# Nine first-layer projections in plain fp32, scan angles in turns, and a new issue order of both mixers

## The chip, the core and the metric

The kernel runs on one core of a Trainium2 chip. The core has five engines that work side by side: TensorE (PE, the matrix engine; its weight loads are shown as PEld), VectorE (DVE), ScalarE (ACT), GpSimd (POOL), and SyncE (SP), which here only issues DMAs. Each engine takes its own instructions strictly in the order in which they stand in its queue, and waits on semaphores where an operand comes from another engine or from a DMA. The metric is the device time of one execution in microseconds (us), as the median of several runs.

## The reference

A two-layer decoder trunk on a sequence of 512 tokens of width 1024, batch 1. Each layer normalises `x`, multiplies it by one wide input projection, feeds slices of the result to three mixers (a sparse attention called NSA, a low-rank attention called MLA, and a diagonal state-space scan called S5), joins them by an output projection, and then runs a gated feed-forward network with a short convolution. Cut to what matters here:

```
cos, sin = rope_angles(positions)
for l in range(DEPTH):                                   # DEPTH = 2
    h = rms_norm(x, attn_norm[l])
    (q_a, k_c, v_c, k_s, v_s, k_w, v_w, gate_a,
     c_q, c_kv, k_r, u) = split(h @ w_in[l])             # 16 column tiles of 128
    o_a = nsa_attention(q_a, k_c, v_c, k_s, v_s, k_w, v_w, gate_a, ...)
    o_b = mla_attention(c_q, c_kv, k_r, cos, sin, ...)
    o_c = s5_ssm(u, ...)
    x = x + concat[rms_norm(o_a), rms_norm(o_b), rms_norm(o_c)] @ w_out[l]
    x = x + conv_ffn(rms_norm(x), ...)
out = rms_norm(x)

# in s5_ssm: the scan's decay is a complex number per group and state
dt = exp(log_dt);  a_bar = exp((a_re + 1j * a_im) * dt)   # angle a_im * dt, up to many turns
```

All data is float32. `rope_angles` needs the sine and cosine of position times frequency; the scan needs the sine and cosine of multiples of `a_im * dt`.

## The kernel before

**Layout.** Activations are kept transposed, features on the 128 partitions and the 512 tokens along the free dimension, so `x` is eight tiles of 128x512. The input projection is 16 tiles of 128 output features, named `u0 u1 ckv krg cq0 cq1 cq2 kc vc ks kw vs vw q0 q1 q2`; each takes eight 128x128 weight blocks, loaded as two halves of 128x512 (256 KB).

**Precision by splitting.** Nearly every large matmul is done in a reduced float format (`fp32r`) on split operands: `split` (lines 224 to 231) writes a rounded `hi` and the rest `lo`; ACT makes `hi` (line 226, or line 229 with a scale), DVE or POOL makes `lo` (line 227, or line 230 with a scale). `mm3` (lines 239 to 242) then adds three products: hi by hi, hi by lo, lo by hi. A weight half is loaded by `wload` into one of three `raw` tiles and split into one of four `wt` tiles; for the input projections POOL makes the weights' `lo` (`win="G"`). A few matmuls are plain float32 on unsplit operands: the sums of squares (line 253), the broadcast of `rstd` (line 271), the transposes, the compression (line 816), and one 128x512 product in `k_rope` (line 764).

**The start.** Eight chunks of `x` are loaded; each is scaled and split at once by `prep_x` (lines 313 to 318), while the halves of the first two projections (`vc`, `kc`) arrive between them. The squares of `x` are added up on POOL (line 294), PE sums them over partitions (line 253), DVE runs the short chain of `rstd_` (lines 256 to 268), PE broadcasts its result (line 271), and ACT copies it to SBUF (line 275). Each finished projection is multiplied by that `rstd` as DVE takes it out of PSUM (lines 687 and 689), so projections may run before `rstd` is known, in a ring of four PSUM banks, but cannot leave PSUM before.

**The tables.** `trig` (lines 300 to 312) brings an angle into -pi to pi: DVE multiplies by 1/(2 pi) and rounds by a magic number (lines 301, 302), subtracts three parts of 2 pi (line 304), clips (line 305); ACT takes the sine of the angle and of half of it (lines 308, 309), and DVE makes the cosine as 1 - 2 sin^2 (lines 310, 311). It is used once for the rotary tables (`rope`, 128x512) and, in `ssm_tables` of each layer, for a 128x16, a 128x256 and two 128x512 tiles. The first layer's tables run at the start of its mixer (task `tab`); the second layer's run inside the first layer's feed-forward network.

**The mixers.** A layer's mixer is a list of tasks. `PLAN0` and `PLAN1` order them: a task with step -1 is issued before the first head; the others are issued at a step of the head pipeline, and some are tied behind a given PE instruction of a head. A head unit (18 in all: 12 NSA units, two per head, then 6 MLA units) goes through `prep`, `scores` (PE, line 519; taken out of PSUM by DVE with a row minimum, line 520; exponentials on ACT, line 523), `scale` (POOL, line 532) and `pv` (transposes on PE, line 544; splits by ACT and DVE, lines 226 and 227; products on PE, line 548). The tasks named here: `cmp0` and `cmp1` compress keys and values, `ca` scores them, `pa0` to `pa3` and `sp0` to `sp3` prepare and spill the scan's matrices by quarters (lines 410 to 427 and 440 to 453, first layer only), `s0` to `s3` run the scan, `w0` to `w7` are the first parts of the output projection. The tile framework's scheduler merges these lists into one queue for each engine, so the final order of an engine is read from the built program, not from the table; `high_priority(offset=cfg["hp"])` moves `rstd_` forward in it.

Of the kernel before, what the change touches and what calls it, by code (L numbers as in the profile page):

```python
# [13 lines left out]
AF = mybir.ActivationFunctionType  # L14
OP = mybir.AluOpType
# [10 lines left out]
PI = float(np.nextafter(np.float32(math.pi), np.float32(0)))  # L26
MAGIC = 1.5 * 2.0 ** 23
# [103 lines left out]
def _pre(names):  # L131
# [3 lines left out]
# The order in which each layer's mixer is issued. An entry is (task, step of the head pipeline, instruction of the  # L135
# tensor engine that it stays behind as (stage, unit) or None); step -1 comes before the first head.
PLAN0 = _pre('vc kc q2 cmp0 q0 tab krg q1 rope cmp1 ks kw pa0 vs sp0 gates pa1 ca sp1 pa2 sp2 pa3 sp3 ') + (
# [3 lines left out]
    ("mlav", 8, None), ("so1", 9, None), ("glu", 11, None), ("mixc", 11, None), ("mixe", 15, None),  # L141
    ("w0", 16, (0, 13)), ("w1", 17, (1, 14)), ("w2", 17, (3, 13)), ("w3", 17, (0, 14)), ("w4", 19, (1, 16)),
    ("w5", 20, (3, 15)))
PLAN1 = _pre('krg q1 kc q0 vc gates q2 cmp0 ks ca u0 kw cp ') + (
# [3 lines left out]
    ("mlav", 8, None), ("glu", 11, None), ("krope", 11, None), ("mixc", 16, None), ("mixe", 16, None),  # L148
    ("w0", 17, (3, 13)), ("w1", 18, (0, 15)), ("w2", 19, (1, 16)), ("w3", 19, (3, 15)), ("w4", 20, (3, 16)))
# [6 lines left out]
def tile_trunk(ctx, tc, xT_in, pos, cst_in, small_in, win, wuq, wuk, wuv, wglu, wout, wup, wdn,  # L156
# [450 lines left out]
    for c in range(8):  # L607
# [4 lines left out]
        for i, at in enumerate(cfg["lead"]):  # L612
            if at == c:
                first[heads2[i % 2]].append(wproj(0, heads2[i % 2], i // 2))
# [708 lines left out]
```

## Time and profile before

| | us |
|---|---|
| median of 3 runs | 1373.47 |
| lowest and highest run | 1370.69, 1375.71 |
| profiled execution: span from first to last instruction | 1372.3 |
| PE busy in it | 1302.4 (95%) |
| DVE, ACT, POOL busy | 856.5 (62%), 638.8 (47%), 724.4 (53%) |
| first rows: first head's scores on PE, and taken out by DVE | 105.5, 112.0 |
| first layer's feed-forward network, roughly | 340 to 725 |
| second layer's mixer, roughly | 725 to 1008 |

The profile is of one execution. Busy time of an engine counts its instructions from start to end; matmuls are pipelined, so one that takes 0.39 us from start to end may be followed 0.23 us later by the next. `PEclk` is the clock that TensorE was granted, as a share of 2.4 GHz; there are two levels, 2.4 and 1.2 GHz, so a mean of 0.75 in a stretch means half of it at each. The idle time shown beside an instruction is that of its engine just before it, with the instruction or DMA that ended it.

### The profile page before, as it was taken

What the parts mean: (1) busy time and instruction counts of PE and PEld (TensorE: products, weight loads), DVE (VectorE), ACT (ScalarE), POOL (GpSimd) and SP (SyncE); (2) the same over time, 40 slices, a digit from 0 to 9 for tenths busy, and PEclk for the clock granted to TensorE, in tenths of its full rate; (3) what the DMA queues carried; (4) which work ended last, traced back from release to release, by engine and by line L of the source; (5) the groups of instructions that cost most, each with busy time, mean ns of one, the idle gap of its engine ahead of it and who ended that gap; (6) DMA issues with size and microseconds to landing.
All of it is one profiled execution on the core that took longest, in us unless ns stands there. A gap on an engine that the chain in (4) does not pass through costs nothing.

```text
span 1372.3 us, 19205 instructions
## 1 busy us (share of the span) xinstructions
PE 1302.4 (95%) x6414; PEld 1079.2 (79%) x6414; DVE 856.5 (62%) x1733; ACT 638.8 (47%) x1322; POOL 724.4 (53%) x722
## 2 busy tenths in 40 slices
PE   7888989998998999999999999999999999999997
PEld 5676777786876888888888887877878888888886
DVE  6988889858695334643466488986764433442455
ACT  4334667754443233423443356886453323332344
POOL 7485546654759155545437665556376315612532
PEclk9989999999999999999999999999999999999998
DMA  6243622212333333443353433121223333333332
GB/s 224 83 131 99 182 85 66 68 62 64 98 99 113 111 95 100 117 124 95 112 173 112 149 124 106 59 60 43 83 85 106 95 100 99 94 92 106 95 94 83
DMA packets 91556, 140.14 MB, mean 102 GB/s; under 512 B 15553, under 2 KB 36545, under 8 KB 91457
## 3 DMA queue, kind: packets, MB, share of 16 engines
q1 hardware_dynamic: 90176, 134.72, 32.2%
q0 software_dynamic: 1280, 4.20, 1.0%
q8 instruction: 50, 0.82, 0.3%
q14 instruction: 50, 0.40, 0.1%
HBM read 125.01 MB, written 15.96 MB: 103 GB/s over the span
## 4 chain that ended last, share of the span: by engine, by line
PE 72%; DVE 19%; issue 3%; POOL 2%; ACT 2%; DMA 2%; SPq 0%; DVEq 0%; POOLq 0%; ACTq 0%
PE bank L240 21%; PE bank L241 20%; PE bank L242 20%; DVE r L227 3%; PE bank L519 2%; PE bank L548 2%; DVE f L520 2%; PE bank L544 2%; DVE r L230 1%; DVE f L304 1%; DVE f L1157 1%; PE bank L271 1%; PE bank L816 1%; PE bank L253 1%; POOL wt L227 1%
## 5 line engine op out<-in xcount | busy, mean ns | idle before, releaser
L240 PE MATMUL bank<-r,wt 128*128 128x512 f32 x1466 | 580.9, 397 | 15.2 <-ACT wt L226 7.3
L241 PE MATMUL bank<-r,wt 128*128 128x512 f32 x1466 | 577.0, 394 | 4.4 <-DVE r L230 3.6
L242 PE MATMUL bank<-r,wt 128*128 128x512 f32 x1466 | 573.4, 394 | 5.1 <-POOL wt L227 5.1
L227 POOL TENSOR_TENSOR wt<-raw,wt 128x512 fp32r<-128x512 f32 (+2 forms) x272 | 355.0, 1309 | 300.1 <-ACT wt L226 291.0
L226 ACT CAST wt<-raw 128x512 fp32r<-128x512 f32 (+2 forms) x398 | 231.0, 584 | 332.5 <-PE bank L241 189.6
L240 PEld LDWEIGHTS bank<-r,wt 128*128 128x128 f32 x1466 | 278.2, 190 | 77.2 <-ACT wt L226 8.9
L242 PEld LDWEIGHTS bank<-r,wt 128*128 128x128 f32 x1466 | 278.0, 190 | 66.1 <-POOL wt L227 8.5
L241 PEld LDWEIGHTS bank<-r,wt 128*128 128x128 f32 x1466 | 278.4, 190 | 62.8 <-DVE r L230 6.5
L227 DVE TENSOR_TENSOR wt<-raw,wt 128x512 fp32r<-128x512 f32 (+3 forms) x126 | 88.9, 709 | 51.7 <-ACT wt L226 51.3
L294 POOL TENSOR_TENSOR f<-f,f 128x512 f32<-128x512 f32 (+1 forms) x53 | 68.0, 1284 | 99.9 <-ACT f L286 98.4
L532 POOL TENSOR_SCALAR f<-f,sml 128x128 f32<-128x128 f32 (+3 forms) x144 | 79.3, 569 | 52.2 <-DVE sml L530 18.0
L227 DVE TENSOR_TENSOR r<-bank,r 128x256 fp32r<-128x256 f32 (+4 forms) x196 | 90.2, 476 | 24.2 <-ACT r L226 23.0
L1182 DVE TENSOR_TENSOR f<-bank,f 128x512 f32<-128x512 f32 x44 | 30.3, 690 | 112.6 <-PE bank L242 103.1
L1188 POOL TENSOR_TENSOR f<-f,f 128x512 f32<-128x512 f32 x44 | 58.0, 1320 | 74.6 <-ACT f L1187 74.6
L523 ACT ACTIVATE f<-f,sml 128x384 f32<-128x384 f32 (+3 forms) x144 | 80.6, 560 | 32.5 <-DVE sml L520 31.6
L226 ACT CAST r<-bank 128x256 fp32r<-128x256 f32 (+4 forms) x196 | 79.0, 417 | 31.8 <-PE bank L544 15.7
L548 PE MATMUL bank<-r,r 128*128 128x512 f32 (+3 forms) x288 | 82.1, 353 | 10.4 <-DVE r L227 7.5
L519 PE MATMUL bank<-r,r 128*128 128x128 f32 (+3 forms) x336 | 79.3, 339 | 9.8 <-DVE sml L520 9.5
L226 ACT CAST r<-f 128x512 fp32r<-128x512 f32 (+1 forms) x76 | 46.9, 620 | 80.5 <-DVE f L1189 65.7
L520 DVE CUSTOM_DVE_ANT_0 f<-bank,cst 128x384 f32<-128x384 f32 (+3 forms) x144 | 67.8, 481 | 12.7 <-PE bank L519 11.6
L1189 DVE TENSOR_TENSOR f<-bank,f 128x512 f32<-128x512 f32 x44 | 30.4, 690 | 72.7 <-POOL f L1188 68.9
L1217 DVE TENSOR_TENSOR f<-bank,f 128x512 f32<-128x512 f32 x48 | 32.7, 688 | 65.6 <-PE bank L242 65.5
(225 smaller groups left out, 1549.9 us busy)
## 6 DMA issues: line engine op xcount, KB each, us to landing
raw<-in_wup_dram SPq DMA_DIRECT2D x176, 256.0 KB
raw<-in_wdn_dram SPq DMA_DIRECT2D x72, 256.0 KB
raw<-in_win_dram SPq DMA_DIRECT2D x64, 256.0 KB
f<-pd SPq DMA_DIRECT2D x32, 256.0 KB
raw<-in_wout_dram SPq DMA_DIRECT2D x32, 192.0 KB
f<-in_xT_dram SPq DMA_DIRECT2D x16, 256.0 KB
f<-in_w_dram SPq DMA_DIRECT2D x16, 256.0 KB
pd<-f SPq DMA_DIRECT2D x16, 256.0 KB
```

Of the source, the lines that this page charges most:

```text
L226: A.copy(hi, src)
L227: (E or V).tensor_tensor(lo, src, f32(hi), op=OP.subtract)
L240: PE.matmul(p, lhsT=w[:, 0, o:o + n], rhs=x[:, 0], start=start, stop=False)
L241: PE.matmul(p, lhsT=w[:, 0, o:o + n], rhs=x[:, 1], start=False, stop=False)
L242: PE.matmul(p, lhsT=w[:, 1, o:o + n], rhs=x[:, 0], start=False, stop=stop)
L294: G.tensor_tensor(a, a, q, op=OP.add)
L519: PE.matmul(p[:, :w], lhsT=q[:, i * 128:w], rhs=k[:, :w], start=n == 0, stop=n == len(passes) - 1)
L520: V.tensor_tensor_reduce(out=sm[i], in0=p[:, :w], in1=C("mask")[:, 512 - w:], op0=OP.add, op1=OP.min, scale=1.0, scalar=3.0e38, accum_out= ...
L523: A.activation(sm[i], sm[i], AF.Exp, bias=mx[:, i:i + 1], scale=-1.0, accum_out=su[:, i:i + 1])
L532: G.tensor_scalar(sm[i], sm[i], rs[:, i:i + 1], 1.0, op0=OP.mult, op1=OP.mult)
L548: PE.matmul(o[:, j * 128:], lhsT=v[j], rhs=pr[:, x, :w], start=first and j == 0 and x == 0, stop=last and j == 3 and x == 1)
L1188: G.tensor_tensor(t, t, r_f, op=OP.mult)
```

## The change

Four things change.

1. **Plain fp32 projections.** Nine projections of the first layer (`vc kc q2 q0 krg q1 ks kw vs`, the list `plain`) are computed as one plain float32 matmul for each weight block, on the weight as loaded (`wplain`, straight into a free `f` tile) and on the scaled `x` (`xg`, made by ACT). The other seven, and the second layer, keep `mm3`. The split `hi`, `lo` of `x`, which these need, is now made by `split_x` from `xg`, in program order after `q2`.
2. **Angles in turns.** `turn_trig` takes the scan's angle as a fraction of a circle: DVE rounds by the magic number and subtracts (two instructions), and ACT takes the sine, the absolute value, and the sine of a quarter turn less that value. `trig`, now used for the rotary tables alone, keeps its reduction but takes the cosine in the same way.
3. **Issue order.** `PLAN0` and `PLAN1` are new, `hp` is 0 instead of 50, and the places behind which two late output tiles of the first layer stand differ.
4. **One engine.** The `lo` part of the MLA queries (made by `split` in `proj_q` after line 940; `q="V"`) moves from POOL to DVE, six 128x512 instructions in each layer.

```diff
+TURN = 2 * PI
-PLAN0 = _pre('vc kc q2 cmp0 q0 tab krg q1 rope cmp1 ks kw pa0 vs sp0 gates pa1 ca sp1 pa2 sp2 pa3 sp3 ') + (
+PLAN0 = _pre('vc kc cmp0 tab q0 rope q2 krg cmp1 ks pa0 kw q1 sp0 pa2 gates pa1 vs sp1 ca sp2 pa3 sp3 ') + (
...
-PLAN1 = _pre('krg q1 kc q0 vc gates q2 cmp0 ks ca u0 kw cp ') + (
+PLAN1 = _pre('krg q0 vc gates q2 ks kc cmp0 q1 ca u0 kw ') + (
...
-CFG = dict(plan=(PLAN0, PLAN1), F=dict(main=15, aux=10, side=12), R=dict(main=16, side=3, q=3, pr=2), nraw=3, nw=4, hp=50,
+CFG = dict(plan=(PLAN0, PLAN1), F=dict(main=15, aux=10, side=12), R=dict(main=16, side=3, q=3, pr=2), nraw=3, nw=4, hp=0,
...
+           ... plain=("vc", "kc", "q2", "q0", "krg", "q1", "ks", "kw", "vs"), splitat="q2", ...
-           eng=dict(..., q="G", xadd="V"))
+           eng=dict(..., q="V", xadd="V"))
...
         A.activation(s, ang, AF.Sin)
-        A.activation(k, ang, AF.Sin, scale=0.5)
-        V.tensor_tensor(k, k, k, op=OP.mult)
-        V.tensor_scalar(k, k, -2.0, 1.0, op0=OP.mult, op1=OP.add)
+        A.activation(k, ang, AF.Abs)
+        A.activation(k, k, AF.Sin, bias=quarter, scale=-1.0)
+
+    def turn_trig(u, k, s):
+        V.tensor_scalar(k, u, MAGIC, None, op0=OP.add)
+        V.scalar_tensor_tensor(u, k, MAGIC, u, op0=OP.subtract, op1=OP.subtract)
+        if s is None:
+            return
+        A.activation(s, u, AF.Sin, scale=-TURN)
+        A.activation(k, u, AF.Abs)
+        A.activation(k, k, AF.Sin, bias=quarter, scale=-TURN)
...
-        V.tensor_tensor(th, aim, dt, op=OP.mult)
-        trig(th, kk, None)
+        V.scalar_tensor_tensor(th, aim, 1.0 / (2 * math.pi), dt, op0=OP.mult, op1=OP.mult)
+        turn_trig(th, kk, None)
...
+    def wplain(name, kh):
+        raw = F.get()
+        SY.dma_start(raw, win[0, TILES.index(name), :, kh * 512:(kh + 1) * 512])
+        return raw
+
+    def split_x():
+        for c in range(8):
+            pr = R.get("main")
+            split(xg[c], pr[:, 0], pr[:, 1])
+            hx.append(pr)
+
     for c in range(8):
         xt = F.get()
         SY.dma_start(xt, xT_in[c])
-        prep_x(xt, c, hx, None, 0, "attn")
+        g = F.get()
+        A.activation(g, xt, AF.Identity, scale=S(0, "attn", c))
+        xg.append(g)
...
+            for kh in range(2 if plain else 0):
+                w = first[name].pop(0) if first.get(name) else wplain(name, kh)
+                for k in range(4):
+                    PE.matmul(p, lhsT=w[:, k * 128:(k + 1) * 128], rhs=xg[kh * 4 + k], start=kh + k == 0, stop=kh == 1 and k == 3)
+                F.free(w)
```

How the engines' queues change is read from the built programs. The first place is PE at the end of the first two projections (`vc` in `bank_151`, `kc` in `bank_152`; `ones` is the sum of squares, `bank_153` the third projection; `r` and `wt` are split tiles, `f` plain ones). Before:

```order
L241 MATMUL bank_152<-r_106,wt_130 128x512
L242 MATMUL bank_152<-r_106,wt_130 128x512
L240 MATMUL bank_152<-r_107,wt_130 128x512
L241 MATMUL bank_152<-r_107,wt_130 128x512
L242 MATMUL bank_152<-r_107,wt_130 128x512
L253 MATMUL bank_155<-ones,f_71 128x1 x4
L253 MATMUL bank_155<-ones,f_72 128x1 x4
L242 MATMUL bank_153<-r_100,wt_127 128x512
L240 MATMUL bank_153<-r_101,wt_127 128x512
```

And the same place of the changed program:

```order
L703 MATMUL bank_152<-f_78,f_76 128x512
L703 MATMUL bank_151<-f_80,f_73 128x512
L703 MATMUL bank_152<-f_80,f_76 128x512
L703 MATMUL bank_151<-f_82,f_73 128x512
L703 MATMUL bank_152<-f_82,f_76 128x512
L257 MATMUL bank_155<-ones,f_83 128x1 x4
L257 MATMUL bank_155<-ones,f_84 128x1 x4
L703 MATMUL bank_153<-f_64,f_63 128x512
L703 MATMUL bank_153<-f_68,f_63 128x512
```

The sum of squares stands behind 50 split matmuls before (48 of the two projections and two of the third) and behind 16 plain ones now. The second place is POOL at the start (line 227, now 231: a weight's `lo`; line 294, now 298: the sum of squares). Before:

```order
L227 TENSOR_TENSOR wt_128<-raw_125,wt_128 128x512
L294 TENSOR_TENSOR f_71<-f_71,f_73 128x512
L294 TENSOR_TENSOR f_72<-f_72,f_74 128x512
L227 TENSOR_TENSOR wt_129<-raw_126,wt_129 128x512
L992 MEMSET f_66 128x64 x2
L294 TENSOR_TENSOR f_71<-f_71,f_75 128x512
L294 TENSOR_TENSOR f_72<-f_72,f_76 128x512
L992 MEMSET f_67 128x64 x2
L623 TENSOR_SCALAR smt<-smt 128x2 x2
L227 TENSOR_TENSOR wt_130<-raw_124,wt_130 128x512
```

Changed:

```order
L298 TENSOR_TENSOR f_83<-f_83,f_85 128x512
L298 TENSOR_TENSOR f_84<-f_84,f_86 128x512
L298 TENSOR_TENSOR f_83<-f_83,f_87 128x512
L298 TENSOR_TENSOR f_84<-f_84,f_85 128x512
L650 TENSOR_SCALAR smt<-smt 128x2 x2
L298 TENSOR_TENSOR f_84<-f_84,f_87 128x512
L298 TENSOR_TENSOR f_83<-f_83,f_86 128x512
L231 TENSOR_TENSOR wt_127<-raw_124,wt_127 128x512
L231 TENSOR_TENSOR wt_128<-raw_125,wt_128 128x512
```

No weight split stands among the sums of squares any more. The third place is DVE while it makes the scan's tables and takes projections out of PSUM (`f_98`, `f_92` are the two 128x512 angle tiles, `f_93`, `f_99` their scratch; line 416, now 429, is the scan's first small operand). Before:

```order
L301 TENSOR_SCALAR f_93<-f_92 128x512
L302 TENSOR_SCALAR f_99<-f_99 128x512
L416 TENSOR_SCALAR f_95<-f_95,cst 128x64
L417 TENSOR_SCALAR f_95<-f_95 128x64
L364 TENSOR_TENSOR ar<-f_97,f_96 128x256
L302 TENSOR_SCALAR f_93<-f_93 128x512
L304 SCALAR_TENSOR_TENSOR f_98<-f_99,f_98 128x512
L369 TENSOR_SCALAR sml_139<-ar 128x16
L823 TENSOR_SCALAR f_88<-f_88 128x62
L304 SCALAR_TENSOR_TENSOR f_92<-f_93,f_92 128x512
L687 SCALAR_TENSOR_TENSOR f_85<-bank_152,f_79 128x512
L304 SCALAR_TENSOR_TENSOR f_98<-f_99,f_98 128x512
```

Changed, at about the same place (the second angle tile is made and reduced, lines 399, 317 and 318):

```order
L728 TENSOR_TENSOR f_87<-bank_151,f_85 128x512
L439 TENSOR_TENSOR f_96<-f_95,ais 128x512
L399 SCALAR_TENSOR_TENSOR f_92<-f_95,cst 128x512
L440 TENSOR_TENSOR f_97<-f_97,f_96 128x512
L317 TENSOR_SCALAR f_93<-f_92 128x512
L860 TENSOR_SCALAR f_88<-bank_158,smt 128x62
L318 SCALAR_TENSOR_TENSOR f_92<-f_93,f_92 128x512
L841 TENSOR_TENSOR f_90<-f_86,f_89 64x256 x2
L430 TENSOR_SCALAR f_95<-f_95 128x64
L439 TENSOR_TENSOR f_96<-f_95,ai 128x512
```

Each angle tile now takes two DVE instructions after it is made, where it took six before the sine and two after it; the scan's quarter products (lines 439 and 440) follow sooner. Up to the first head's scores both programs issue the same 11 projections.

## Rows read from the trace of the kernel before

**Rows 1.** The page: the chain that ended last, by engine.

```profile
PE 72%; DVE 19%; issue 3%; POOL 2%; ACT 2%; DMA 2%; SPq 0%; DVEq 0%; POOLq 0%; ACTq 0%
```

**Rows 2.** Busy time by stretch; the first row names the columns.

```profile
core 0: us, PE busy (x) PEld busy (x) DVE busy (x) ACT busy (x) POOL busy (x), PEclk, DMA share, GB/s
...
27.70:112.00 84.30, 73.14 (x363) 60.87 (x363) 77.17 (x157) 29.86 (x51) 55.59 (x63) 0.94 0.37 114
112.00:320.00 208.00, 190.54 (x1071) 158.22 (x1072) 165.65 (x470) 133.84 (x348) 113.60 (x148) 0.96 0.30 90
...
725.00:1008.00 283.00, 270.75 (x1493) 228.38 (x1493) 216.42 (x544) 168.79 (x408) 169.29 (x192) 1.00 0.29 89
```

**Rows 3.** PE's waits from 0 to 112 us: total, times, longest.

```profile
PE bank L829 <- DVE f L828: 3.6, 1, 3.6
PE bank L816 <- DMA f<-in_w_dram: 2.9, 1, 2.9
```

**Rows 4.** Timeline of PE and DVE: start, duration, engine, line, operation.

```profile
25.85 1.84 PE L253 MATMUL bank<-ones,f 128*128 128x1 f32 x16
...
27.72 0.16 DVE L256 TENSOR_SCALAR sml<-bank 128x4 f32<-128x4 f32 x1 [5.64 <-PE bank L253]
...
112.04 0.28 DVE L520 CUSTOM_DVE_ANT_0 f<-bank,cst 128x128 f32<-128x128 f32 x1
```

**Rows 5.** Timeline of PE: split matmuls early, and in the feed-forward network.

```profile
11.07 0.63 PE L240 MATMUL bank<-r,wt 128*128 128x512 f32 x1
...
12.53 0.39 PE L242 MATMUL bank<-r,wt 128*128 128x512 f32 x1
...
500.15 0.39 PE L240 MATMUL bank<-r,wt 128*128 128x512 f32 x1
...
500.83 0.39 PE L240 MATMUL bank<-r,wt 128*128 128x512 f32 x1
```

**Rows 6.** The plain 128x512 matmul: durations (ns least/median/most), and its place.

```profile
L764 PE MATMUL bank<-f,cst x4: 592/592/594, 226.8 to 896.6; 128*128 128x512 f32 x4
...
896.20 1.02 PE L764 MATMUL bank<-f,cst 128*128 128x512 f32 x2
```

**Rows 7.** A piece of the chain: start, duration, what (22 short plain matmuls).

```profile
85.22 3.06 PE bank L816 x22
```

**Rows 8.** DVE groups, 27.7 to 112 us: busy us, mean ns, idle before.

```profile
L304 DVE SCALAR_TENSOR_TENSOR f<-f,f 128x512 f32<-128x512 f32 x9 | 7.2, 804 | 0.0
...
L310 DVE TENSOR_TENSOR f<-f 128x512 f32<-128x512 f32 x3 | 3.5, 1174 | 0.1
...
L305 DVE TENSOR_SCALAR f<-f 128x512 f32<-128x512 f32 x3 | 2.1, 713 | 0.0
...
L301 DVE TENSOR_SCALAR f<-f 128x512 f32<-128x512 f32 x3 | 1.6, 533 | 0.0
...
L311 DVE TENSOR_SCALAR f<-f 128x512 f32<-128x512 f32 x3 | 1.4, 482 | 0.0
L304 DVE SCALAR_TENSOR_TENSOR f<-f,f 128x256 f32<-128x256 f32 x3 | 1.4, 468 | 0.0
```

**Rows 9.** POOL's weight splits, 0 to 112 us: busy us, mean ns, idle before.

```profile
L227 POOL TENSOR_TENSOR wt<-raw,wt 128x512 fp32r<-128x512 f32 x26 | 36.9, 1428 | 15.1 <-ACT wt L226 14.8
```

**Rows 10.** Timelines of DVE and POOL at one weight split.

```profile
33.57 0.10 DVE L304 SCALAR_TENSOR_TENSOR sml<-sml,sml 128x16 f32<-128x16 f32 x1
...
33.93 1.25 DVE L304 SCALAR_TENSOR_TENSOR sml<-sml,sml 128x16 f32<-128x16 f32 x1
...
33.67 1.48 POOL L227 TENSOR_TENSOR wt<-raw,wt 128x512 fp32r<-128x512 f32 x1 [1.68 <-ACT wt L226]
```

**Rows 11.** Line 227 on two engines: durations (ns least/median/most), span, shapes.

```profile
L227 DVE TENSOR_TENSOR r<-f,r x46: 678/693/1639, 189.5 to 1332.1; 128x512 fp32r<-128x512 f32 x46
L227 POOL TENSOR_TENSOR r<-f,r x30: 1262/1300/1775, 74.6 to 944.7; 128x512 fp32r<-128x512 f32 x22, 64x512 fp32r<-64x512 f32 x8
```

**Rows 12.** Scores on PE: durations (ns least/median/most), first and last start, shapes.

```profile
L519 PE MATMUL bank<-r,r x336: 218/336/667, 105.5 to 943.6; 128*128 128x128 f32 x48, 128*128 128x384 f32 x47, 128*128 128x512 f32 x37, 128*128 128x256 f32 x36
```

More of the change, by code (lines that the diff above doesn't have):

```diff
@@ L132, in _pre @@
     return tuple((n, -1, None) for n in names.split())
[L137 removed]
[3 rows of a table removed]
[L141 to L144 removed]
[3 rows of a table removed]
[L148 to L152 removed]
+PLAN0 = _pre('vc kc cmp0 tab q0 rope q2 krg cmp1 ks pa0 kw q1 sp0 pa2 gates pa1 vs sp1 ca sp2 pa3 sp3 ') + (
[3 rows of a table added]
+    ("so1", 9, None), ("mlav", 8, None), ("glu", 9, None), ("mixc", 11, (0, 10)), ("mixe", 15, (1, 14)),
+    ("w0", 17, (2, 14)), ("w1", 17, (1, 14)), ("w2", 17, (1, 16)), ("w3", 17, None), ("w5", 20, (3, 15)),
+    ("w4", 18, (1, 16)))
+PLAN1 = _pre('krg q0 vc gates q2 ks kc cmp0 q1 ca u0 kw ') + (
[4 rows of a table added]
+    ("krope", 11, None), ("mixc", 11, None), ("mixe", 16, None), ("w0", 19, (3, 13)), ("w1", 19, (0, 15)),
+    ("w2", 19, (1, 17)), ("w3", 19, (3, 15)), ("w4", 20, (3, 16)))
+CFG = dict(plan=(PLAN0, PLAN1), F=dict(main=15, aux=10, side=12), R=dict(main=16, side=3, q=3, pr=2), nraw=3, nw=4, hp=0,
+           order=(2, 1, 3, 0), rings=dict(), tabs=2, plain=("vc", "kc", "q2", "q0", "krg", "q1", "ks", "kw", "vs"), splitat="q2", lead=(0, 0, 3, 4), units=('NNNNNNMMMMMM', 'NNNNNNMMMMMM'), rest=((-9, -1, -5, -7, -7, -1, -1, -1), (-1, -1, -3, -1, -1, -1, -1, -1)),
+           eng=dict(wo="G", mix="G", klo="G", csub="G", gel="G", win="G", wup="G", wdn="V", wo2="V", q="V", xadd="V"))
 @with_exitstack
@@ L216, in tile_trunk @@
     A.activation(sml(1), ones, AF.Exp)
+    quarter = mk([128, 1], "quarter")
+    V.memset(quarter, PI / 2)
     bd = mk([128, 3, 64], "bd")
@@ L356, in ssm_tables @@
         kvb = kv[:, :, None].to_broadcast(big)
+        V.tensor_scalar(th, th, -1.0, None, op0=OP.mult)
         b0, b1, b2 = F.get(), F.get(), F.get()
@@ L385, in ssm_tables @@
             an, kb, sb = F.get(), F.get(), F.get()
[L386 to L388 removed]
+            V.scalar_tensor_tensor(shp(an, 8, 64), red[:, 15, h * 8:h * 8 + 8][:, :, None].to_broadcast([128, 8, 64]), -1.0,
+                                   C("cv")[:, None, :].to_broadcast([128, 8, 64]), op0=OP.mult, op1=OP.mult)
+            turn_trig(an, kb, sb)
             for q in range(2):
@@ L605, in tile_trunk @@
     heads2 = [n for n, _, _ in cfg["plan"][0] if n in TILES][:2]
-    first, xts = {n: [] for n in heads2}, []
+    first, xts, xg = {n: [] for n in heads2}, [], []
+    def wplain(name, kh):
[7 more added lines that the diff above has]
+            hx.append(pr)
     for c in range(8):
@@ L613, in tile_trunk @@
             if at == c:
-                first[heads2[i % 2]].append(wproj(0, heads2[i % 2], i // 2))
+                first[heads2[i % 2]].append(wplain(heads2[i % 2], i // 2))
     SY.dma_start(smt[:, 0, 8:], small_in[:, 0, 8:])
@@ L669, in proj @@
             p = ps(ring)
-            for kh in range(2):
+            plain = l == 0 and name in cfg["plain"]
+            if not (plain or hx):
+                split_x()
+            for kh in range(2 if plain else 0):
[3 more added lines that the diff above has]
+                F.free(w)
+            if plain and name == cfg["plain"][-1]:
+                F.free(*xg)
+            if plain and name == cfg["splitat"]:
+                split_x()
+            for kh in range(0 if plain else 2):
                 w = first[name].pop(0) if first.get(name) else wproj(l, name, kh)
```

7 lines of the change are left out of this document (1 added, 6 removed), and 13 rows, old and new, of tables (PLAN0, PLAN1).

## The prediction

> **What bounds the kernel now.** I read the chain that ended last first: PE holds 72% of it, DVE 19%, and no other engine over 2% [rows 1]. Taken alone this says that PE work is what counts, and the change adds PE work. So the second view has to be the busy time by stretch, which shows where the chain isn't PE. From 27.7 us, when the normalising chain of the first layer begins, to 112.0, when the first head's scores leave PSUM, DVE is busy 77.2 of 84.3 us while PE is busy 73.1 and at a granted clock of 0.94 [rows 2, 4]. DVE is the fuller engine there, and at 0.94 PE spent some of the stretch at the lower of its two clock levels. From 112 to 320 and in the second layer's mixer (725 to 1008) PE is busy 92% and 96%, DVE 80% and 76% [rows 2]: both are well filled, neither alone is the bound. In the two feed-forward networks PE never stops, and the change touches nothing there but the second layer's angle tables. So the stretch to work out is the first 112 us; the rest mostly moves with it.
>
> **PE work added.** A split product is three matmuls. In a steady stretch three of them start within 500.83 - 500.15 = 0.68 us [rows 5]. The plain 128x512 product stands in the trace too: line 764, two calls, four records, so two passes a call, each 592 ns from start to end; both together take 1.02, so the second starts 0.43 after the first and a call holds PE for 0.86 us [rows 6]. Nine projections of eight blocks are 72 products: 72 x (0.86 - 0.68) = 13 us more on PE. Nothing hides this: it is the price of the change.
>
> The Trainium skill weighs in against the change here: FP8 and Floating Point Precision, TensorE Precision Notes (under Matmul Precision), says that true FP32 goes through the array in four passes. The trace shows two records of double length, 0.86 us, where four passes at the pace of the split ones would be 4 x 0.227 = 0.91 us; by the page the added work would be 72 x 0.23 = 16 us, 3 us more than I take. The row decides.
>
> **DVE work removed before the first scores.** Three angle tiles of the first layer lose most of their reduction. Of the 128x512 rows, line 304 goes from nine to three (6 x 0.80 = 4.8 us), 305 from three to one (1.4), 301 likewise (1.1), 310 and 311 vanish (3.5 and 1.4), and the 128x256 rows of 304 vanish (1.4) [rows 8]: 13.6 us, with the narrower and shorter ones left out. In come two rounding instructions at the price of 301 (1.1), two subtractions at that of 304 (1.6), and a 128x256 pair (about 0.7): 3.4. Net 10 us. The order puts a few of the scan's quarter products ahead of the first scores that stood behind them: two 128x512 and four short ones, 3 us at the prices of line 304, work that is saved later. ACT gets an absolute value for each tile; it is busy 29.9 of 84.3 us [rows 2], which covers that.
>
> **POOL work removed.** 18 weight halves are no longer split, 1.43 us each on POOL [rows 9], some 26 us. POOL isn't the bound, but it holds DVE up: a 128x16 instruction that takes 0.10 us takes 1.25 beside a weight split that began at 33.67 [rows 10], and ends with it. About 13 of the 18 fall after 27.7 us. Each gives DVE between nothing and 1.15 us back; I take 0.7, so 9 us, since not each of them meets an instruction that must wait.
>
> **The two paths to the first scores.** DVE: the sum of squares now stands behind 16 plain products rather than 50 split ones, and no weight split stands among POOL's additions. PE starts at about 5 us, when the first chunk and weight half are there; 16 x 0.86 = 13.7 us, and about 3 us more for the first six microseconds at the lower of the two clock levels (a matmul takes 0.63 at 11.07 us and 0.39 at 12.53 [rows 5]): 21.7 us. The sum of squares takes 1.84 [rows 4], so DVE starts its chain at 23.6 instead of 27.7. From there it has 77.2 - 10 - 9 + 3 = 61 us of work; with its 7.1 us of idle time before kept it would reach the first scores at 23.6 + 68 = 92 us.
>
> PE: 21.7 + 1.8, then 56 plain products (48), two split projections of 24 matmuls (48 x 0.227 = 10.9), 64 passes of the compression at 3.06 / 22 = 0.14 (8.9) [rows 7], and some 6 us, an estimate, for the compressed scores, transposes and spills, all short: 97 us. So PE becomes the bound up to the first scores, and the whole price of the plain products is inside this figure. Its waits must be added. Before, PE was idle 84.3 - 73.1 = 11.2 us in this stretch, most of it in single waits for the gelu of the compression and for its weights [rows 3]; since PE now has more of its own to do while DVE is ahead of it, I keep 4 of them: first scores at 101 us, DVE taking them out at once, against 112.0. That is 11 us earlier, with bounds: no idle time at all gives 15, all 11.2 kept gives 4.
>
> **What follows.** The tasks behind the first scores are the same in number, so I carry the 11 us to the end of the mixer. The queries' `lo` costs DVE 12 x 0.69 us, and takes 12 x 1.30 from POOL [rows 11]; DVE has 42 us of idle time from 112 to 320 and 67 in the second mixer [rows 2], so I cost it at nothing; if that cover is gone it is 4 us for a layer. The new order (`hp`, the steps, the anchors) removes and adds nothing; what it is worth isn't in the trace. Its bounds are PE's idle time in the two mixers, 17 and 12 us [rows 2], to the gain, and some 8 us to the loss, as much as two or three waits of the kind in [rows 3] more in each layer; I take zero. The second layer's tables save DVE some 10 us too, inside the feed-forward network, where PE doesn't wait for DVE for long: 1 us. Sum: 11 + 1 = 12 us off the profiled 1372.3. The median of the runs is 1.2 above that span, so 1361.5 us.
>
> **Rivals.** (a) *PE's idle time stays and its added work is simply added.* If what keeps PE waiting is not DVE's load but latency (the gelu chain, the DMA of the compression's weights [rows 3], the clock lost after each), then 11.2 us of idle and about 5 us at half clock remain, and the first scores come on PE at 97 + 16 = 113 instead of 105.5 [rows 12]: 7.5 us later, 1381. It decides from 14 us of waits on. For it: PE holds 72% of the chain. Against it: DVE's fullness, and that PE's longer queue covers just such waits. (b) *The early gain is lost on the way.* The head pipeline from 112 to 320 is a chain over four engines, and new places of its tasks can cost what the start wins; with DVE's added 4 us in each layer the time stays at 1372. For it: DVE 80% busy there; against: the same work, started sooner. (c) *The order wins too.* If it takes half of the mixers' PE idle time, 15 us more: 1347. (d) That the plain products don't run at 0.86: at the lower clock level each costs twice that. With PE fed without a break from 7 us on I see no reason; it would be part of (a).
>
> **How the numbers follow.** Forecast 0.55 (its own range 1357 to 1370, from the bounds of 4 and 15 us), (a) 0.1, (b) 0.18, (c) 0.17. The 80% range takes in most of (b) and (c): 1348 to 1375. A difference counts from 0.3%, 4.1 us, about what a measurement of this kernel can tell. Faster: nearly all of the forecast and (c), some of (b): 0.72. Same: most of (b): 0.17. Slower: (a) and a little of (b): 0.11.
>
> **What would show it.** In the changed profile: plain products of two records, 0.86 us apart; DVE's normalising chain at 23 to 25 us; the first scores taken out at 97 to 108; PE busier than DVE from 27.7 to there, and at a higher granted clock; POOL's busy time down by some 40 us in all; the two feed-forward networks as long as before. Wrong if the first scores are early and the first mixer still ends at 320 to 335 (then (b)), or if they come at 112 or later with PE idle as before (then (a)).

## The result

The changed kernel takes 1354.7 us (median of 4 runs, 1352.1 to 1356.9) against 1373.3 for the kernel before (1370.7 to 1375.7): ratio 0.986, 95% interval 0.984 to 0.988. That is 18.6 us less, where the prediction said 12. The profiled execution's span fell from 1372.3 to 1354.1 us.

First the page of the changed kernel: busy time and share of each engine, and the chain that ended last, by engine.

```profile
PE 1302.1 (96%) x6342; PEld 1057.8 (78%) x6342; DVE 818.1 (60%) x1702; ACT 634.1 (47%) x1317; POOL 683.2 (50%) x692
...
PE 74%; DVE 14%; issue 3%; DMA 3%; POOL 3%; ACT 2%; SPq 1%; DVEq 0%; POOLq 0%; ACTq 0%
```

DVE's share of the chain fell from 19% [rows 1] to 14%. PE is busy as long as before (1302.4), although its work has grown; how both can be true is the main point below. POOL was busy 724.4 before.

Busy time by stretch in the changed kernel, columns as in [rows 2]: from the first normalising chain to the first scores, from there to the last scores of layer 0, and the second layer's mixer.

```profile
23.40:101.60 78.20, 75.80 (x302) 45.50 (x302) 58.81 (x140) 23.80 (x42) 38.88 (x59) 1.00 0.38 116
101.60:270.00 168.40, 157.98 (x946) 131.84 (x945) 142.53 (x433) 119.33 (x319) 100.03 (x128) 1.00 0.34 101
696.00:1000.00 304.00, 288.71 (x1567) 243.20 (x1566) 223.85 (x563) 173.60 (x417) 175.75 (x195) 0.99 0.30 91
```

In the first stretch PE is now the fuller engine (75.8 of 78.2 us; 73.1 of 84.3 before), DVE went from 77.2 to 58.8, and the granted clock from 0.94 to 1.00. The head stage behind it (the second row) ran at 0.95 in the kernel before, at 1.00 now:

```profile
112.00:287.40 175.40, 158.64 (x907) 132.16 (x908) 146.83 (x429) 117.06 (x312) 101.25 (x134) 0.95 0.31 93
```

PE's waits in the changed kernel from 0 to 101.6 us (total, times, longest). The 5.3 is the time before PE's first product; behind it, the long ones of [rows 3] are gone or shorter:

```profile
PE bank L703 <- ACT f L636: 5.3, 1, 5.3
PE bank L868 <- DVE f L867: 1.6, 1, 1.6
PE bank L703 <- DMA f<-in_win_dram: 0.8, 1, 0.8
```

The timeline of the changed kernel, for [rows 4] and for the pace of the plain product [rows 6]: the sums of squares on PE, DVE's first step behind them, seven plain records, the first scores taken out.

```profile
21.46 1.86 PE L257 MATMUL bank<-ones,f 128*128 128x1 f32 x16
...
23.36 0.16 DVE L260 TENSOR_SCALAR sml<-bank 128x4 f32<-128x4 f32 x1 [1.49 <-PE bank L257]
...
31.03 3.17 PE L703 MATMUL bank<-f,f 128*128 128x512 f32 x7
...
101.63 0.27 DVE L533 CUSTOM_DVE_ANT_0 f<-bank,cst 128x128 f32<-128x128 f32 x1
```

Where the 18 us came from, by stage. The times are the first or last instruction of a kind in each trace (DVE's scores, its gate evacuations, its last residual addition of the first network).

| stage, us | before | after | gain |
|---|---|---|---|
| start to first scores, layer 0 | 112.0 | 101.6 | 10.4 |
| to its last scores | 175.3 | 168.4 | 6.9 |
| to the first gate of network 0 | 73.6 | 70.3 | 3.3 |
| network 0 | 359.1 | 355.7 | 3.4 |
| to first scores, layer 1 | 58.2 | 64.7 | -6.5 |
| to its last scores | 166.4 | 170.2 | -3.8 |
| to network 1 | 73.1 | 68.9 | 4.2 |
| network 1, to the end | 354.5 | 354.4 | 0.1 |

The first line is about what I predicted (11). The others are not: I had 0 for the mixers and 1 for network 0.

A second ledger tells what kind of time it was. For each trace I summed PE's idle time, and the time for which its clock records grant half speed, both up to 20 us before the end (the last microseconds differ by chance). The rest is the span less these 20 us, less the idle time and less half of the half-speed time, that is, PE's work at full speed. The kernels are those of the next section.

| kernel | span | PE idle | at half speed | rest |
|---|---|---|---|---|
| before | 1372.3 | 60.1 | 34.1 | 1275.2 |
| after | 1354.1 | 42.3 | 10.2 | 1286.7 |
| before, new order only | 1387.2 | 65.2 | 58.0 | 1273.0 |
| after, old order | 1364.3 | 45.9 | 23.9 | 1286.5 |
| after, all products split | 1359.2 | 54.2 | 20.5 | 1274.8 |
| after, angles in radians | 1378.2 | 51.0 | 44.4 | 1285.0 |
| after, old plan of layer 0 | 1370.8 | 50.3 | 30.7 | 1285.2 |
| after, old first part of it | 1382.4 | 56.1 | 44.4 | 1284.1 |
| after, five plain projections | 1362.7 | 51.9 | 23.9 | 1278.9 |
| after, old plan of layer 1, `q` on POOL | 1350.0 | 40.2 | 6.8 | 1286.4 |

From before to after: 11.5 us more work, 17.8 us less idle time, and 23.9 us less at half speed, worth 12.0. Sum: -18.3 us. Over these kernels the rest goes with the number of plain products alone, to within 2.6 us; the other differences between them are waiting and clock. (Idle time that falls into half-speed time is counted in both, so the ledger is rough where waits are long; the slow matmuls of the first 12 us [rows 5] stand in no clock record and count as work.)

What a wait does to the clock is seen in the kernel before, at its first head. Timeline of PE (idle time before an instruction and its releaser in brackets), then two stretches:

```profile
115.06 0.42 PE L519 MATMUL bank<-r,r 128*128 128x128 f32 x2
118.59 0.80 PE L519 MATMUL bank<-r,r 128*128 128x256 f32 x2 [3.11 <-DVE sml L520]
...
121.24 0.63 PE L240 MATMUL bank<-r,wt 128*128 128x512 f32 x1
121.67 0.63 PE L241 MATMUL bank<-r,wt 128*128 128x512 f32 x1
```

```profile
112.00:118.00 6.00, 3.08 (x15) 2.24 (x15) 5.27 (x14) 3.43 (x10) 4.49 (x7) 1.00 0.30 90
118.00:125.00 7.00, 6.00 (x15) 4.62 (x16) 5.95 (x18) 2.01 (x7) 2.21 (x2) 0.51 0.32 90
```

PE waited 3.11 us for DVE to empty a score bank. From 118.0, just before the wait ended, its clock stood at the lower level (1.2 GHz) for 7 us: a split matmul starts every 0.43 us there, not every 0.227 [rows 5]. At half speed 7 us lose some 3 more, as much as the wait.

### The profile page after: what moved, and what is told of

It is laid out like the page before. It is cut to its first block, busy times and chain, and to the rows that moved or that the text cites. A ratio compares the mean times of both kernels' runs of the same rounds, so it can differ in the third digit from the quotient of the medians.

```text
span 1354.1 us, 18970 instructions
## 1 busy us (share of the span) xinstructions
PE 1302.1 (96%) x6342; PEld 1057.8 (78%) x6342; DVE 818.1 (60%) x1702; ACT 634.1 (47%) x1317; POOL 683.2 (50%) x692
## 4 chain that ended last, share of the span: by engine, by line
PE 74%; DVE 14%; issue 3%; DMA 3%; POOL 3%; ACT 2%; SPq 1%; DVEq 0%; POOLq 0%; ACTq 0%
PE bank L244 21%; PE bank L245 20%; PE bank L246 20%; PE bank L532 3%; DVE r L231 2%; PE bank L703 2%; PE bank L561 2%; PE bank L557 2%; DVE f L533 1%; DVE r L234 1%; DVE f L1196 1%; PE bank L855 1%; PE bank L275 1%; PE bank L257 1%; DVE wt L231 1%
## 5 line engine op out<-in xcount | busy, mean ns | idle before, releaser
L244 PE MATMUL bank<-r,wt 128*128 128x512 f32 x1394 | 548.7, 395 | 7.5 <-DVE f L1195 3.2
L245 PE MATMUL bank<-r,wt 128*128 128x512 f32 x1394 | 545.1, 392 | 0.2 <-DVE r L234 0.2
L246 PE MATMUL bank<-r,wt 128*128 128x512 f32 x1394 | 541.5, 392 | 3.2 <-POOL wt L231 2.8
L231 POOL TENSOR_TENSOR wt<-raw,wt 128x512 fp32r<-128x512 f32 (+2 forms) x254 | 328.3, 1296 | 297.3 <-ACT wt L230 292.5
L230 ACT CAST wt<-raw 128x512 fp32r<-128x512 f32 (+3 forms) x380 | 220.4, 583 | 313.4 <-PE bank L245 180.4
L244 PEld LDWEIGHTS bank<-r,wt 128*128 128x128 f32 x1394 | 262.4, 188 | 66.3 <-DVE f L1195 4.2
L246 PEld LDWEIGHTS bank<-r,wt 128*128 128x128 f32 x1394 | 262.4, 188 | 59.8 <-POOL wt L231 4.8
L245 PEld LDWEIGHTS bank<-r,wt 128*128 128x128 f32 x1394 | 262.7, 188 | 52.9 <-DVE r L234 0.9
L536 ACT ACTIVATE f<-f,sml 128x128 f32<-128x128 f32 (+3 forms) x144 | 80.8, 562 | 31.0 <-DVE sml L533 27.7
L230 ACT CAST r<-bank 128x256 fp32r<-128x256 f32 (+4 forms) x196 | 78.2, 417 | 27.8 <-PE bank L557 13.7
L230 ACT CAST r<-f 128x512 fp32r<-128x512 f32 (+1 forms) x84 | 51.5, 619 | 84.1 <-DVE f L1228 68.0
L532 PE MATMUL bank<-r,r 128*128 128x128 f32 (+3 forms) x336 | 76.2, 336 | 7.3 <-DVE sml L533 6.2
L231 DVE TENSOR_TENSOR r<-f,r 128x512 fp32r<-128x512 f32 x66 | 58.3, 887 | 29.2 <-ACT r L230 28.8
```

Source lines behind the costliest of these rows:

```text
L230: A.copy(hi, src)
L231: (E or V).tensor_tensor(lo, src, f32(hi), op=OP.subtract)
L244: PE.matmul(p, lhsT=w[:, 0, o:o + n], rhs=x[:, 0], start=start, stop=False)
L245: PE.matmul(p, lhsT=w[:, 0, o:o + n], rhs=x[:, 1], start=False, stop=False)
L246: PE.matmul(p, lhsT=w[:, 1, o:o + n], rhs=x[:, 0], start=False, stop=stop)
L532: PE.matmul(p[:, :w], lhsT=q[:, i * 128:w], rhs=k[:, :w], start=n == 0, stop=n == len(passes) - 1)
```

## The experiments

The kernels of one batch ran on one chip beside the kernel before (1373.1 to 1374.2 there). "First scores" and the stages are from each kernel's profile, one execution.

**The order alone, on the old loads.** With it go the offset and the engine of the queries' `lo`.

```
 (kernel before)
-PLAN0 = _pre('vc kc q2 cmp0 q0 tab krg ...   PLAN1 = _pre('krg q1 kc ...   hp=50  rest ((-7, ...  q="G"
+PLAN0 = _pre('vc kc cmp0 tab q0 rope q2 ...  PLAN1 = _pre('krg q0 vc ...   hp=0   rest ((-9, ...  q="V"
```

> The kernel before with nothing but the new issue order: both plans, the places of the last output projections, the priority offset 0, and the queries' remainder on VectorE. Projections stay split and angles stay in radians. Theory (two parts: the early relief of VectorE and GpSimd brings the first scores forward by 10 us, and the order is worth some 7 us behind them): first scores where they were, 110 to 114 us; from there to the last score of layer 0 168 us instead of 175; the whole 1366 us (1363 to 1369). Rival A (the order is worth nothing, the shorter head pipeline comes from the early relief too): 1373, the head pipeline 175 us. Rival B (the order does nearly all of it, the first stage included): 1358 or less, first scores at 105 or earlier.

1392.7 us, ratio 1.013 (1.011 to 1.015): 18.5 us slower, further off than any of the three answers. First scores at 113.4, head stage 190.7 us at a clock of 0.92:

```profile
113.40:304.10 190.70, 171.17 (x965) 143.85 (x965) 153.00 (x444) 121.19 (x321) 103.32 (x141) 0.92 0.31 95
```

Two of PE's waits before the first scores (lines are one higher than in the kernel before):

```profile
PE bank L830 <- DVE f L829: 4.0, 1, 4.0
PE bank L817 <- DVE f L311: 3.3, 1, 3.3
```

Line 311 there is the squaring in the old angle routine (line 310 before). The new order puts the tables ahead of the compression, so with the long reduction the compression's products wait behind it. But PE's idle time up to the first scores is 20.4 us, as in the kernel before (20.5), and they come only 1.4 us later. Most of the loss lies in the head stage, which is 15.3 us longer: 6.8 by the clock, 2.8 of idle time and 5.7 of work that moved into it. How the order brings this about isn't shown. It isn't worth a number of its own.

**The loads alone, in the old order.** The reverse: the changed kernel with both old plans, the old `rest`, `hp=50` and `q="G"`.

> The kernel after with the issue order of before: plain fp32 projections and the angles in turns, but both old plans, the old places of the last output projections, the old priority offset, and the queries' remainder on GpSimd. Theory: first scores at 101 to 104 us, the head pipeline of layer 0 back at 173 to 176 us, the whole 1361.5 us, as forecast for the change without a worth of the order (1359 to 1364). Rival A (order worth nothing): 1355. Rival B (order does it all): 1370 or more, first scores at 108 or later.

1366.9 us against 1374.2 beside it, ratio 0.996 (0.994 to 0.997): a gain of 7.3 us, not the 12 of the theory. First scores at 106.1, but 182.7 us of head stage at 0.95:

```profile
106.10:288.80 182.70, 165.60 (x935) 137.84 (x934) 142.32 (x428) 118.66 (x316) 104.20 (x133) 0.95 0.31 93
```

By the last scores the early gain is gone (288.8 us, 287.4 before), as in the prediction's rival (b), but not for its reason: the tasks' places are the old ones here, and PE's idle and half-speed time in the stage are as before (17.1 us for 16.8, and 17 each). What grew by 7 us is the work done in it, and the first gate comes 4.5 us sooner again. Against the changed kernel this stage has 6.7 us more idle time and 8.5 us more lost by the clock. The chain began only at 27.3 us, with plain products too:

```profile
19.80 5.74 PE L702 MATMUL bank<-f,f 128*128 128x512 f32 x13
25.38 1.84 PE L256 MATMUL bank<-ones,f 128*128 128x1 f32 x16
```

The sums of squares stand behind 4 us more of plain products here than in the changed kernel, which has them at 21.46.

**Split products, in the new order.** `plain=()`, and the head of the kernel (scaled input split chunk by chunk, weight halves split) as before.

> The kernel after with the nine projections as split products again (three matmuls a block, weight halves split on ScalarE and GpSimd, the scaled input split chunk by chunk at the start); angles in turns and the new order stay. Theory: TensorE has 13 us less to do, but VectorE is the fuller engine again: it keeps the 10 us that the angles save and loses the 9 us that the missing weight splits gave it, so first scores at 104 to 108 us and the whole 1359 us (1356 to 1364). Rival C (TensorE's work is what counts everywhere): 13 us fewer, 1342. Rival D (plain is the whole gain of the first stage): first scores at 111 or later, 1366 or more.

1364.9 us, ratio 0.993 (0.991 to 0.995), first scores at 108.5: just above both of the theory's ranges. Leaving out the plain products' extra work makes the kernel 10 us slower, so rival C falls. PE's work is 11.9 us less and its idle time 11.9 more in the ledger, with 10.3 us more at half speed. (Its profile is an execution 4 us faster than the median.)

**Radians, in the new order.** `trig` and `ssm_tables` as before; everything else as in the changed kernel.

> The kernel after with the angles reduced as before (radians, three constants, a clamp; cosine from a squared half-angle sine) in both layers' scan tables and the rotary tables; plain projections and the new order stay. Theory: VectorE gets 10 us of work back before the first scores; by the prediction's two sums TensorE reaches them at 97 and VectorE at 92 without this, so VectorE is at 102 and bounds with its waits: first scores at 104 to 107 us, the whole 1359 us (1357 to 1362). Rival E (TensorE alone bounds the first stage now, VectorE's load is covered): 101.6 as in the kernel after, 1354.7. Rival D (the angles are the whole gain of the first stage): 110 or later, 1364 or more.

1372.2 us, ratio 0.999 (0.998 to 1.001): the whole gain is gone, as rival D has it for the whole; first scores at 109.1, between the theory's range and the rival's. Its profile is the longest of its 12 executions, 24 us above the changed kernel's span where the medians are 17.5 apart: 7.5 of the 24 are in the first stage, 13.4 in the head stage (181.8 us at 0.93) and 3.2 in network 0. Of the 13.4 the clock takes 11.9 and idle time 4.7, less 3.2 of work. One of the waits there is for the scan's data, and the clock falls at it. Wait and timeline of that kernel:

```profile
PE bank L496 <- DMA f<-pd: 3.3, 1, 3.3
```

```profile
143.50 1.68 PE L496 MATMUL bank<-f,f 128*128 128x64 f32 x8 [3.30 <-DMA f<-pd]
...
147.13 0.63 PE L246 MATMUL bank<-r,wt 128*128 128x512 f32 x1
147.55 0.63 PE L244 MATMUL bank<-r,wt 128*128 128x512 f32 x1
```

The tables' sines and cosines go through `pd` to the scan, so late tables can make the scan late; this wait was not traced back to them. The longest low stretch, 13.7 us from 174.5 on, stands by other waits, of 1.1 and 0.7 us.

**The old plan of layer 0.**

```
 (kernel after)
-PLAN0 = _pre('vc kc cmp0 tab q0 rope q2 krg ...'),  rest=((-9, -1, -5, -7, -7, ...
+PLAN0 = _pre('vc kc q2 cmp0 q0 tab krg q1 ...'),    rest=((-7, -1, -1, -5, -7, ...
```

> The kernel after with the first layer's plan of before (and the old places of its last output projections); the second layer's plan, the offset 0 and the queries' remainder on VectorE stay. Theory K (an order fits one set of loads: with the old one TensorE waits for score banks again, and each wait of a few us is followed by TensorE's clock at its lower level): head stage of layer 0 180 us or more with a mean granted clock of 0.95 or less, the whole 1366 (1362 to 1370). Rival S (the worth of the order is its own, as the one-by-one sum has it: old order before 175, so 175 here): first scores at 101 to 104, 1360 to 1362 and a clock near 1.00.

1371.2 us, ratio 0.998 (0.997 to 1.000); first scores 106.4, head stage 181.2 at 0.96: the whole is 1 us above theory K's range, the clock a little above its bound. Rival S falls: the new order of layer 0 is worth 16.5 us on the new loads, while both new orders together cost 18.5 on the old.

```profile
106.40:287.60 181.20, 163.93 (x935) 136.02 (x935) 146.13 (x434) 118.76 (x317) 96.31 (x127) 0.96 0.31 94
```

**Only the first part of that plan.** The entries ahead of the first head as before, those among the heads as after.

> The kernel after with only the first part of the first layer's plan as before (what stands ahead of the first head); the places of the tasks among the heads, the anchors, the last output projections and the second layer's plan stay new. With the whole old plan of that layer the first scores came at 106.4 us, the head stage took 181.1 us at a clock of 0.95 or less, and the whole 1371. Theory U (the order ahead of the first head decides both: with VectorE late there, score banks and scan data are late in the head stage too, TensorE waits and its clock falls): first scores 105 to 107, head stage 178 or more, 1366 to 1371. Rival V (the two parts decide their own stages): first scores 105 to 107, head stage 168 to 171, 1357 to 1361.

1380.5 us, ratio 1.005 (1.003 to 1.007): first scores 107.8, head stage 180.9. Theory U's direction holds and rival V falls: putting back what is issued ahead of the first head is enough to lengthen the head stage by 12 us. It is worse than the whole old plan by 9 us (above U's range), and 10 were lost between the last scores and the first network (79.1 us against 69.2). The other half, the new first part with the old places among the heads, wasn't run.

**The old plan of layer 1; `q` on POOL; `hp` 50.** Three kernels, each with one entry of the changed kernel put back.

> The kernel after with the second layer's plan of before, nothing else changed. Both kernels with that plan so far reached that layer's first scores 58.2 us after the first feed-forward network, the ones with the new plan 64.5 to 64.8; from the last score to the next network they took 73.1 against 68.9. But these two also had the priority offset 50 and the queries' remainder on GpSimd. Theory P (the plan sets these times): 58 and 73 us, head stage 166 to 168 instead of 170, the whole 1348 to 1350. Rival H (the offset or the remainder's engine sets them): 64.7 and 68.9 as in the kernel after, 1354.7.

> The kernel after with the queries' remainder (12 subtractions in all) back on GpSimd. The prediction valued this at nothing, 4 us for a layer if VectorE's idle time doesn't cover it. Theory: 1353 to 1357. Rival (GpSimd scales the heads, and with 1.3 us more for each subtraction the transposes wait for it): 1359 or more, with new waits of TensorE for GpSimd's scaled heads.

> The kernel after with the priority offset of the normalising chains back at 50. In the run with the old order VectorE began the first chain at 27.3 us although the plain products were there, and at 23.4 in both kernels with plain products and offset 0. Theory (the offset, or the order, not the plain products alone, brought the chain forward; TensorE bounds the stage anyway): chain at 23 to 27, first scores at 101 to 105, the whole 1354 to 1359. Rival H (the offset also holds the second layer's 58.2 us between the network and its first scores): 1349 or less.

1354.1 (0.984 to 0.988), 1355.4 (0.985 to 0.989) and 1354.5 us (0.985 to 0.989): none can be told from the changed kernel. Theory P was half right: the plan does set the stage before layer 1's first scores (58.6 us, not 64.7), but the heads then took 174.4 and gave most of it back, and the stage behind them stayed at 69.4 us. The new plan does more PE work in that stage, it doesn't wait there (changed kernel, then old plan):

```profile
696.00:760.70 64.70, 64.29 (x334) 54.51 (x333) 32.52 (x61) 22.47 (x39) 47.06 (x44) 1.00 0.42 130
```

```profile
696.90:755.50 58.60, 58.40 (x309) 49.81 (x308) 32.00 (x56) 21.70 (x37) 42.56 (x40) 1.00 0.41 129
```

With `hp` 50 the chain still began at 23.2 us, so it isn't the offset that delayed it in the old order. With `q` on POOL the time is in its theory's range.

**Five plain projections.** `plain=("vc", "kc", "q0", "q2", "krg")`.

> The kernel after with only the first five projections plain (vc, kc, q0, q2, krg) and q1, ks, kw, vs split. TensorE has 4 x 8 x 0.18 = 6 us less to do before the first scores, GpSimd 8 weight splits (11 us) more. Theory of the prediction (TensorE bounds the first stage, its plain products are the price): first scores 3 to 5 us earlier, 97 to 99, and 1350. Rival D (VectorE and GpSimd still decide, as the run without plain products says): first scores at 102 to 105 and 1356 to 1360.

1369.7 us, ratio 0.996 (0.994 to 0.998): 15 us slower than the changed kernel, where the theory had 5 less, and beyond rival D. The work fell by 7.8 us in the ledger, and first scores came 4.8 us later, at 106.4: from 23.4 us on, 5.8 more of idle time and 3.4 of clock, less 4.4 of work. (Here too the profiled execution is shorter than the median, by 5 us.) PE's waits before them:

```profile
PE bank L868 <- DVE f L867: 3.7, 1, 3.7
PE bank L453 <- DVE f L885: 2.5, 1, 2.5
```

With less to do, PE is early at the compression (at 56.1 us, not 61.6) and waits 3.7 us for its gelu, where the changed kernel waits 1.6. So PE bounds the stage only while it has enough queued. DVE was fuller too (64.8 us, not 58.8), with eight more weight splits on POOL; how much each did wasn't separated.

**The price of a wait.** In network 1, where PE otherwise hardly waits, blocks of idle multiplications hold DVE (work added that changes no output).

```
+                hold = {2: 17, 5: 19, 10: 21, 13: 24}.get(m, 0) if l == 1 else 0
...
+                    for _ in range(hold):
+                        V.tensor_tensor(z, z, z, op=OP.mult)
...
                 V.tensor_tensor(gp, pg, r_f, op=OP.mult)
```

> The kernel after with four blocks of 17, 19, 21 and 24 idle multiplications of 128x512 on VectorE in the second feed-forward network, at units 2, 5, 10 and 13, where TensorE otherwise never waits. By 0.69 us each they hold VectorE for 11.7, 13.1, 14.5 and 16.6 us, and the two banks ahead cover one unit (10.9 us): estimated waits of TensorE of 1, 2, 4 and 6 us, 13 us in all. Theory K (a wait of two or three us is followed by TensorE's clock at its lower level, for 3.4 us or 6.8 as seen after such waits in the first mixer): granted clock 0.5 behind the two or three longest, and the network longer than the sum of its waits by 1.7 or 3.4 us for each, some 5 to 9 us; the whole 1354 + 13 + 7 = 1374. Rival W (a wait costs what it lasts): longer by the waits alone, 1367, the clock as before.

1390.6 us, 35.9 above the changed kernel. The waits were not where I wanted them: the multiplications ran between the small steps of the normalising chain ahead of the network, and took 0.88 us each in the mean. So the sizes missed, but the price can be read. Its waits from 990 us on:

```profile
PE bank L275 <- DVE sml L272: 13.0, 2, 10.1
PE bank L244 <- DVE f L1235: 4.2, 2, 2.3
PE bank L244 <- ACT wt L230: 2.8, 1, 2.8
PE bank L245 <- DVE r L234: 2.5, 1, 2.5
PE bank L244 <- DVE f L1228: 2.1, 1, 2.1
```

Nearly the same work to the end, changed kernel and then this one, and one stretch behind a wait:

```profile
990.00:1354.00 364.00, 354.36 (x1647) 296.51 (x1645) 161.94 (x242) 134.41 (x231) 147.18 (x118) 0.99 0.33 96
```

```profile
990.00:1386.10 396.10, 364.39 (x1641) 302.47 (x1639) 221.59 (x319) 134.27 (x231) 153.23 (x117) 0.95 0.30 88
...
1030.90:1034.30 3.40, 3.40 (x10) 2.66 (x9) 3.40 (x6) 1.85 (x4) 0.96 (x1) 0.51 0.02 5
```

Idle time grew from 9.6 to 31.7 us, by 22.1, and the matmuls (1641, for 1647) were busy 10.0 us longer. So 22 us of waits cost 32: 1.45 us for each, a mean over very unequal waits, of which one of 10.1 us is nearly half. Rival W falls.

**A version made of these.** The changed kernel with the old plan of layer 1 and `q` on POOL.

> The kernel after with the second layer's plan of before and the queries' remainder on GpSimd. Each alone moved the whole by less than can be told, but the profile of the first reached the second layer's first scores 6 us sooner and lost 4 of them in the head stage (174.4 us), and that of the other had a head stage of 166.9 instead of 170.2. Theory (the two add up): first scores 58.5 us after the network, head stage 167, 1348 to 1351. Rival (what one stage wins the next loses): 1353 to 1356.

1351.0 us, ratio 0.985 (0.983 to 0.986), within the theory's range: 58.3 us to layer 1's first scores, heads 166.5. Against the kernel before it is faster; against the changed one it is lower by 3.7 us, but the two intervals overlap and they weren't run side by side, so that stays open.

## Why the prediction was right, and where it was not

The time lies below the forecast's own range (1357 to 1370), between it and rival (c)'s 1347; only the wide range holds it. The account of the first stage came out, that of the rest did not.

*Which stretch, and which engine.* Right for the first 10 us. DVE was the fuller engine ahead of the first scores, and its load fell to 58.8 us there, where I had 61. That "the rest mostly moves with it" was not so.

*13 us of plain products.* Right: 7 records in 3.17 us are 0.43 apart, 0.86 a product, and the ledger's rest grows by 11.5 (before to after) or 11.9 (split to plain in the new order), 0.16 a product. The Trainium skill states four passes for true FP32 (FP8 and Floating Point Precision, TensorE Precision Notes). At the pace of the split ones that would have been 16, an estimate; the measured 0.86 is 3.8 times 0.227, and the measurement decides.

*The chain at 23.6.* It began at 23.4, but I gave the reason as the plain products alone. With them and the old order it began at 27.3 (26.2 with the old plan of layer 0 alone): the place of the sums of squares in PE's queue is the other half.

*First scores at 101.* 101.6. PE was idle 2.4 us in the stretch, where I had kept 4, and busy 75.8, where my terms sum to 73.8: two small misses that cancel, which is luck. I put the 101 down to the loads; by the runs it takes plain products, turns and order together. Any one put back gives 106 to 109.

*"I carry the 11 us to the end" and "I take zero" for the order.* This is the step that failed. On the old order the new loads win 5.9 us at the first scores and 7.3 at the end; on the new order they win 38 (1392.7 to 1354.7). The order by itself costs 18.5, beyond the 8 that I gave as its bound, and on the new loads it wins 12. The zero was a mean of things that don't add: in the changed kernel layer 0 won 10.2 us behind the first scores and layer 1 lost 6.1.

| median, us | split, radians | plain only | turns only | both |
|---|---|---|---|---|
| old order | 1373 to 1374 | - | - | 1366.9 |
| new order | 1392.7 | 1372.2 | 1364.9 | 1354.7 |

*PE's waits outside the first stretch.* I read the clock of 0.94 in the first stretch, but in [rows 2] I passed over the 0.96 from 112 to 320, and bounded the order by PE's idle time alone (17 us in that stretch). The half-speed time in the old head stage was 17.1 us, worth 8.5, and all of it went. A wait's price was the term that was mis-sized: 1.45 of its length in the run with held DVE, where I had bounded the order by the length alone. The gain of 6.9 us in that stage is 8.5 of clock and 6.3 of idle time, less 7.9 of work that moved into it.

*Layer 1's tables, 1 us.* 3.4. Network 0 took 358.9 to 360.2 us in the profiles with radians (before, new order only, radians in the new order) and 354.7 to 356.0 in those with turns. In the kernel before PE waits 4.1 us there for POOL's weight splits, the longest followed by half speed:

```profile
400.38 0.50 PE L242 MATMUL bank<-r,wt 128*128 128x512 f32 x1 [2.28 <-POOL wt L227]
...
402.30 0.63 PE L242 MATMUL bank<-r,wt 128*128 128x512 f32 x1
402.73 0.63 PE L240 MATMUL bank<-r,wt 128*128 128x512 f32 x1
```

The changed kernel has 2.5 us of such waits there, the longest 1.85, and no half speed behind it. The half speed isn't what tells the two kinds apart: the profiles of four kernels with turns have such a stretch in this network too (that of split products, from 398 us on, in a network of 355.3). What the kernels with turns share is less idle time of PE, 2.8 to 4.4 us against 5.8 to 6.7 with radians. Why POOL's splits come later with radians isn't shown; [rows 10] shows DVE held beside a POOL split, not the reverse.

*What would show it.* POOL's busy time fell by 41 us (40 said), network 1 is as long as before, and the clock in the first stretch rose to 1.00. Rival (a) didn't happen. A loss like (b)'s in the head stage came with the old places of its tasks, not with new ones, and (c) is what happened in layer 0 alone.

## What to carry to other kernels

An issue order is fitted to the lengths of the operations in it: price a change of loads and a change of order together, and test them crossed, since a new order can be a loss on the old loads (18.5 us here). Where PE is the busy engine, count its waits at about one and a half times their length (1.45 here, from one run), and read the granted clock stage by stage, not only where the waits are longest. Added PE work can pay where it takes work off the engines that PE waits for: with split products again, PE had 11.9 us less to do and 11.9 us more idle time, and the kernel was 10 us slower. Whether PE's fuller queue or the lighter POOL and DVE did more wasn't separated.

## What the runs showed of the hardware that was not expected

- In all 14 profiles, up to the last 20 us, each stretch of PE's clock at its lower level began during or just behind waits of PE, from a single one of 10.1 us (held DVE) down to one of 1.0 (old plan of layer 1, at 987 us) or a pair of 0.8 and 0.5 (kernel before, from 193.5 to 196.4 us). The stretches lasted 3 to 14 us, with PE busy again for most of them. Not each wait does it, and its own length doesn't decide: the changed kernel's 1.85 us before line 246 at 388 us has no slow stretch behind it, while two waits of 0.9 and 1.4 us at 297 and 299 us have one, from 300 on. With `q` on POOL the same wait of 1.85 at the same place has one. What does decide stays open. The changed kernel, then the one with `q` on POOL:

```profile
389.85 0.50 PE L246 MATMUL bank<-r,wt 128*128 128x512 f32 x1 [1.85 <-POOL wt L231]
390.19 0.40 PE L244 MATMUL bank<-r,wt 128*128 128x512 f32 x1
390.42 0.39 PE L245 MATMUL bank<-r,wt 128*128 128x512 f32 x1
```

```profile
389.20 0.50 PE L246 MATMUL bank<-r,wt 128*128 128x512 f32 x1 [1.85 <-POOL wt L231]
...
390.11 0.63 PE L246 MATMUL bank<-r,wt 128*128 128x512 f32 x1
390.54 0.63 PE L244 MATMUL bank<-r,wt 128*128 128x512 f32 x1
```

- At the lower level a split 128x512 matmul starts every 0.43 us (121.24 to 121.67) against 0.227.
- The same order with other loads moved the time by 38 us (1354.7 to 1392.7), and the same loads with other orders by 12 to 26 (1354.7 to 1366.9 and 1380.5), while PE's work at full speed differs by 14 us (the plain products, to the other side) and by 3 in the ledger: the kernels differ by waits and clock.
